# Four parts of the second layer's modulation are computed in the second layer's mixing in place of the first feed-forward

## The chip, the cores and the metric

The kernel runs on one core of one Trainium2 chip. The metric is the time of one execution on the device, in microseconds (us); lower is better. TensorE is PE, VectorE DVE, ScalarE ACT, GpSimd POOL and SyncE SP. PEld is the loading of weights into PE, beside its matmuls. Operands of PE are 32 bits wide.

## The reference, cut to what matters

Two layers work on a latent stream of 512 tokens and a context of 256, each token with 1024 features. A layer first makes six vectors per stream, its modulation, out of one small matrix product: SiLU(c) times a matrix of 1024 x 6144. Then it mixes tokens, and then it runs a feed-forward. The last layer does not update the context.

```python
sh_a, sc_a, ga_a, sh_f, sc_f, ga_f = ada_params(c, w_ada[i], b_ada[i])      # parts 0 to 5; likewise from c_ctx
h = rmsnorm(x, g_mix[i]) * (1.0 + sc_a) + sh_a                              # parts 1 and 0
y, yc = token_mixer(h, hc, ...)         # Fourier mixing, retention and neighbourhood attention, beside one another
x = x + ga_a * y                                                            # part 2
x = x + ga_f * swiglu(rmsnorm(x, g_ffn[i]) * (1.0 + sc_f) + sh_f, w1[i], w3[i], w2[i])    # parts 4, 3, 5
```

In the second layer parts 0 and 1 are needed for both streams, before its mixing starts. Parts 2 to 5 are needed for the latent stream alone: part 2 at its output projection, 3 and 4 at the norm of its feed-forward, 5 in the feed-forward's output.

## The kernel before, in words

Every large product is made three times, to keep 32-bit accuracy. Both operands are split into a high half in a reduced format (a cast on ACT) and a low half (the difference, on POOL or DVE), and PE adds high x high, low x high and high x low (`mm3`, lines 398 to 400). A weight chunk is thus loaded raw by SP, cast on ACT (line 183), subtracted on POOL or DVE (line 188), and only then used. The feed-forward uses a seven-product scheme on 2x2 blocks, so DVE also combines weight blocks (lines 225 to 229) and results (lines 1592 to 1658), and multiplies the two branches into the gated chunks `g` (lines 1634, 1635, 1461, 1462).

`WeightStream` is one list of all weights in the order of their use. It has buffers of one size: a raw chunk takes one, a split chunk of 1024 columns two, one of 512 columns one. `max_raws` limits the raw ones, `max_parts` the split ones and `SLOTS` their sum; 12 such buffers exist, and tables (rotary tables, attention bias, the SiLU tables) take the others. `issue` starts loads on SP's queue in the list's order while buffers are free. `split` handles the next entry; `get` hands a chunk to PE's work, and `done` frees it and lets the stream go on (`pump`). An entry can also be a unit of modulation: when its turn comes its raw buffer goes onto a list of waiting callbacks, and `flush`, which `get` calls, runs those whose time has come. That time is counted in planned PE time (`k.pe`). If the stream needs an entry that isn't issued yet, `flush(True)` runs all waiting callbacks at once.

For the second layer a unit is (part, i), a load of 512 KB with 128 of a part's 1024 features transposed onto partitions, and its callback `ada_dve` (lines 517 to 535) makes one pass on DVE per stream: multiply 128x1024 with the SiLU table of the stream, and sum (line 522, with an accumulator read behind it). After the eighth unit of a part the bias is added (`ada_bias`). For the first layer the products of parts 2 to 5 are made on PE (line 545), as units among the chunks of the first mixing.

`weights_of` (in `build`) places the units: `spread(units, lo, hi)` puts them evenly behind entries lo to hi of a layer's list. The list of the second layer's mixing has 37 chunks: four for the retention values (`rv`, 0 to 3), six for rotary queries and keys (`rq`, `rk`), three gates, six queries and keys and four values of the attention, two Fourier inputs, four transform tables, and eight output chunks (29 to 36).

The order of PE's work in the mixing is written out beforehand: `beside` interleaves the projections with the chain of retention (scores two items ahead of their values), readout and attention, by planned PE time and the offsets in `MIX`. Engines take their instructions in program order. In the retention each score tile goes from PE to DVE (times the decay, line 874), ACT (high half, line 931), DVE or POOL (low half, line 932) and back to PE. In the attention it goes through DVE (line 1076), ACT (exponential), DVE (lines 1118, 1119), PE (transpose), and ACT and DVE (lines 403, 404).

Of the kernel before, what the change touches and what calls it, by code (L numbers as in the profile page):

```python
# [14 lines left out]
NK = 8  # L15
# [24 lines left out]
DMA_WAIT = 8000.0  # L40
# [61 lines left out]
class WeightStream:  # L102
# [88 lines left out]
    def split(self):  # L191

        task = self.tasks[self.n_split]
        key, what, u = task
        size = self.need(task)
        if isinstance(what, Job):
            self.combine(what, key)
        else:
            raw = self.raw.pop(u)
            if what is not None:  # L200
                self.pending.append((what, raw, self.when[u] + DMA_WAIT if key[1] == 0 else 0.0))
            else:
                self.put(key, raw, raw.shape[-1])
                self.n_raw -= 1
            del raw
        self.size[key] = size
        self.n_parts += size
        self.n_split += 1
        self.issue()
# [101 lines left out]
def pieces(st):  # L311

    c0, n = st
    cut = min(max(NLAT - c0, 0), n)
    for s, lo, hi in ((0, 0, cut), (1, cut, n)):
        if hi > lo:
            yield s, slice(c0 + lo, c0 + hi), slice(lo, hi)
# [26 lines left out]
def run(*gens):  # L344
    for g in gens:
        for _ in g:
            pass


class Kern:  # L350
# [168 lines left out]
    def ada_dve(self, raw, layer, part, i):  # L519

        for s in range(1 if layer == DEPTH - 1 and part > 1 else 2):
            self.nc.vector.tensor_tensor_reduce(  # L522
                out=self.tmp(mybir.dt.bfloat16, D, "adj"),
                in0=raw,
                in1=self.tabs[("silu", s)],
                scale=1.0,
                scalar=0.0,
                op0=OP.mult,
                op1=OP.add,
                accum_out=self.mod[:, layer, part, s, i : i + 1],  # L530
            )
        if i == NK - 1:
            self.ada_bias(layer, part, lambda s: self.mod[:, layer, part, s, :])
            if (layer, part) == (DEPTH - 1, 5):
                self.tabs.clear()

    def ada(self, raw, part, half, u):
        nc = self.nc
# [497 lines left out]
    def na_evac_k(self, dst):  # L1036
# [14 lines left out]
        return f  # L1051

    def neighbours(self, layer, nqk, v, y, with_ctx, spans, nv_time, finish):

        nc = self.nc
# [130 lines left out]
        for i in range(len(items) + lag):  # L1186
            if i < len(items):
                h, b = items[i]
                if b == 0:
                    if h % 2 == 0:  # L1190
                        yield spans[h // 2] + (per,)
                        y[h // 2] = self.act(name="yn")
                    begin(h)
                yield score(h, b)
            if SL <= i < len(items) + SL:
                scale(*items[i - SL])
            if i >= lag:
                h, b = items[i - lag]
                if b == 1 and h > 0:
                    if h == 1:  # L1200
                        yield (nv_time, spans[0][1], per / 2)
                    yield values(h - 1, False)
                    if with_ctx:
                        yield values(h - 1, True)
                    if h % 2 == 0:
                        finish(h // 2 - 1)
                    parts(0)
                yield transp(h, b)
                if b > 0 or h == 0:
                    parts(b)  # L1210
        yield values(5, False)
        if with_ctx:
            yield values(5, True)
        finish(2)
        head.clear()

# [96 lines left out]
            for ps, w, m, st in waiting:  # L1313
                yield from self.products(ps, w, src, st, order[a:b], order)

    def residual(self, keys, src, x, layer, part, streams, after, norm, order, n, waiting, hook=None, paces=(1, 2, 2, 2), raws=3):

        nc = self.nc

        def put(ps, m, st):  # L1320
            for s, sl, at in pieces(st):
                xs = x[m][:, sl]
                nc.vector.scalar_tensor_tensor(
                    xs, ps[:, at], self.mod[:, layer, part, s, m : m + 1], xs, op0=OP.mult, op1=OP.add
                )
            after(m, st)

        def one(w, m, st, last, steps=0):
            ps = self.ps("res")
            run(self.products(ps, w, src, st, order, order))  # L1330
            if steps:
                norm.step(steps)
            put(ps, m, st)
            if last:
                self.w.done(keys[m])

        held = {}
        late = waiting[-1][2] + 1
        for ps, w, m, st in waiting:
            if hook:  # L1340
                hook()
            run(self.products(ps, w, src, st, order[n:], order))
            put(ps, m, st)
            if st is streams[-1]:
                self.w.done(keys[m])
        waiting.clear()
        del ps, w
        for m in range(late, NK):
            w = self.w.get(keys[m])
            if hook:  # L1350
                hook()
            if m < 4:
                for st in streams:
                    one(w, m, st, st is streams[-1])
            else:
                one(w, m, streams[0], False)
                held[m] = w
        self.w.max_raws = raws
        nc.scalar.activation(self.warm, self.eps, AF.Sqrt)
        for (m, w), n in zip(held.items(), paces):  # L1360
            one(w, m, streams[1], True, n)


class FeedForward:
# [351 lines left out]
    def finish(self, after, norm, hook=None):  # L1716

        k, q = self.k, len(self.parts) - 1
        size = self.parts[q][1]
        g = [[self.chunk(q, i, p) for i in range(2 * size)] for p in range(2)]  # L1720
        k.w.spare = 0
        k.w.max_raws, k.w.max_parts = 3, 8
        keys = [("w2", self.layer, q, m) for m in range(NK)]
        order = sorted(range(2 * size), key=lambda i: i % size == size - 1)
        waiting = []
        run(k.residual_ahead(keys, 3, g, self.out, order, [2 * size - 2], waiting, hook))
        k.residual(keys, g, self.x, self.layer, 5, self.out, after, norm, order, 2 * size - 2, waiting, hook)
        self.big = self.more = None


def build(tc, a, out, ctx, dbg=None, opts=None):
    k = Kern(ctx, tc, a, out, dbg)
# [5 lines left out]
    w = k.w = WeightStream(k, 3, 8)  # L1738
# [3 lines left out]
    def weights_of(layer):  # L1742
        lat_only = layer == DEPTH - 1
        main, between = [], {}

        def add(n, *idx, ap=None):
            main.append(((n, layer) + idx, a["w_" + n][(layer,) + idx] if ap is None else ap))

        for u in range(4):
            add("rv", u)  # L1750
        for c in range(3):
            add("rq", c)
            add("rk", c)
        for c in range(3):
            add("rg", c)
        for c in range(3):
            add("nq", c)
            add("nk", c)
            if c == 0:
                for u in range(4):  # L1760
                    add("nv", u)
        for c in range(2):
            add("f", c)
        for t in range(5 - lat_only):
            add("dft", t, ap=a["dft"][t] if t < 4 else a["dftc"])
        for m in range(NK):
            add("out", m)
        n_mix = len(main)

        def spread(units, lo, hi):  # L1770
            for i in range(lo, hi):
                n = len(units) * (i - lo) // (hi - lo), len(units) * (i + 1 - lo) // (hi - lo)
                between.setdefault(i, []).extend(units[n[0] : n[1]])

        steps = ffn[layer].order
        if layer == 0:
            spread([(layer, p, u) for p in range(2, 6) for u in range(NK)], 6, n_mix - 4)
        if layer + 1 < DEPTH:
            spread([(layer + 1, p, u) for p in range(6) for u in range(NK)], n_mix + 30, n_mix + len(steps) - 18)
        for i, (key, ap) in enumerate(main):  # L1780
            w.add(key, ap)
            for q in between.get(i, []):
                k.ada_unit(*q)
        for i, (job, p) in enumerate(steps):
            ffn[layer].add_weights(job, p)
            for q in between.get(n_mix + i, []):
                k.ada_unit(*q)
# [8 lines left out]
    x = [k.act(name="x") for _ in range(NK)]  # L1796
# [75 lines left out]
    for layer in range(DEPTH):  # L1872
        last = layer == DEPTH - 1
# [12 lines left out]
        for i, _ in enumerate(k.proj_v([("rv", layer, u) for u in range(4)], h, rv, norms, 3 if layer else 6)):  # L1886
            k.pe += 3 * 384 * NCOL
            if layer == 0 and i % 4 == 1:
                next(strips)
        w.SLOTS = 10  # L1890
        qk, nqk, u, wf = {}, {}, [None] * 2, []
        y, yn = [None] * 8, [None] * 3
        ysp = [[None] * 8, [None] * 8]
# [68 lines left out]
        outs, order, waiting = [("out", layer, m) for m in range(NK)], (2, 3, 4, 0, 1, 5, 6, 7), []  # L1962
# [48 lines left out]
        x = []  # L2011
# [236 lines left out]
```

## Time and profile before

| | us |
|---|---|
| three runs: lowest, median, highest | 1699.99, 1701.46, 1704.0 |
| the profiled execution, its own time | 1700.14 |
| its span, first to last instruction | 1698.4 |
| PE busy in the span | 1601.1 (94%) |
| DVE busy in the span | 1178.8 (69%) |
| POOL, ACT busy | 818.6 (48%), 741.9 (44%) |

The first layer's mixing ends near 450 us, its feed-forward runs to about 980, the second layer's mixing from there to about 1310, and the second feed-forward to the end. The second layer's modulation passes on DVE run from 532.6 to 928.2 us. The mean granted clock of TensorE over the span is 0.982 of full speed. A share of busy time over the whole span mixes stages with different limits, so the rows below go by stretches.

### The profile page before, as it was taken

To read this page: it belongs to the slowest core of one execution; us is meant where nothing else is said; L and a number is where in the kernel's file an instruction comes from. 1 tells how busy PE (TensorE), PEld (TensorE's weight loads), DVE (VectorE), ACT (ScalarE), POOL (GpSimd) and SP (SyncE) were. 2 spreads that over 40 slices of the span, in tenths; PEclk is the share of its full clock that TensorE was granted. 3 is DMA by queue.
4 is the path that set the end of the run, shared out by engine and by line. 5 is a ranking of instruction groups with operands and counts; after the bars stand their busy time and mean duration, and the time that the engine had idled before them with its cause. 6 is when DMAs were issued, how large, how long until landed. Compare 5 with 4: busy or idle time off the path is not lost. (4 is left out here: it accounts for less than half of the span.)

```text
span 1698.4 us, 26272 instructions
## 1 busy us (share of the span) xinstructions
PE 1601.1 (94%) x9730; PEld 1449.0 (85%) x9730; DVE 1178.8 (69%) x2054; ACT 741.9 (44%) x1437; POOL 818.6 (48%) x601
## 2 busy tenths in 40 slices
PE   6989999999979998999999999999999799999996
PEld 4867788888979987899999997779789789999996
DVE  6866566773777899586766776665666876766685
ACT  5534444653553223242332554444554544344343
POOL 3443232123375556465555623444125676666672
PEclk9999999999989999999999999999999899999998
DMA  9364253353023343434443345422232132332322
GB/s 355 139 199 138 67 160 97 119 170 130 26 76 111 103 134 120 129 125 137 149 137 118 127 161 163 135 73 74 80 131 81 60 115 75 111 114 76 94 87 69
DMA packets 76384, 202.28 MB, mean 119 GB/s; under 512 B 12704, under 2 KB 19488, under 8 KB 75872
## 3 DMA queue, kind: packets, MB, share of 16 engines
q1 hardware_dynamic: 76256, 200.60, 36.5%
q8 instruction: 77, 1.26, 0.3%
q14 instruction: 51, 0.42, 0.1%
HBM read 184.25 MB, written 11.80 MB: 115 GB/s over the span
## 5 line engine op out<-in xcount | busy, mean ns | idle before, releaser
L188 POOL TENSOR_TENSOR wp<-wr,wp 128x512 fp32r<-128x512 f32 (+1 forms) x336 | 465.7, 1399 | 311.0 <-ACT wp L183 306.2
L398 PE MATMUL f<-hp,wp 128*128 128x384 f32 (+1 forms) x1232 | 386.8, 314 | 14.8 <-DVE U L1599 4.2
L399 PE MATMUL f<-hp,wp 128*128 128x384 f32 (+1 forms) x1232 | 387.1, 314 | 10.8 <-DVE wp L188 6.2
L400 PE MATMUL f<-hp,wp 128*128 128x384 f32 (+1 forms) x1232 | 385.2, 313 | 4.0 <-POOL hp L1524 4.0
L183 ACT CAST wp<-wr 128x512 fp32r<-128x512 f32 (+1 forms) x360 | 213.3, 609 | 309.4 <-PE f L400 118.5
L188 POOL TENSOR_TENSOR wl<-wr,wh 128x1024 fp32r<-128x1024 f32 (+2 forms) x75 | 163.8, 2188 | 346.4 <-ACT wh L183 266.4
L398 PEld LDWEIGHTS f<-hp,wp 128*128 128x128 f32 x1232 | 238.0, 193 | 18.8 <-issue 8.2
L399 PEld LDWEIGHTS f<-hp,wp 128*128 128x128 f32 x1232 | 238.4, 193 | 15.3 <-POOL wp L188 8.5
L400 PEld LDWEIGHTS f<-hp,wp 128*128 128x128 f32 x1232 | 238.1, 193 | 5.1 <-POOL hp L1524 5.1
L398 PE MATMUL proj<-h,wh 128*128 128x512 f32 (+1 forms) x456 | 165.0, 362 | 1.0 <-DVE v L404 1.0
L398 PE MATMUL f<-g,wp 128*128 128x512 f32 (+1 forms) x468 | 160.5, 343 | 5.4 <-ACT g L1461 5.4
L400 PE MATMUL f<-g,wp 128*128 128x512 f32 (+1 forms) x468 | 160.5, 343 | 0.0
L399 PE MATMUL f<-g,wp 128*128 128x512 f32 (+1 forms) x468 | 160.3, 342 | 0.0
L399 PE MATMUL proj<-h,wl 128*128 128x512 f32 (+1 forms) x456 | 159.1, 349 | 0.7 <-POOL wl L188 0.7
L400 PE MATMUL proj<-h,wh 128*128 128x512 f32 (+1 forms) x456 | 158.9, 348 | 0.0
L1658 DVE SCALAR_TENSOR_TENSOR x<-f,mod,x 128x512 f32<-128x512 f32 (+1 forms) x130 | 79.0, 622 | 69.5 <-PE f L400 69.3
L398 PEld LDWEIGHTS proj<-h,wh 128*128 128x128 f32 x456 | 86.6, 190 | 25.5 <-issue 6.6
L522 DVE CUSTOM_DVE_ANT_0 adj<-wr,tab 128x1024 bf16<-128x1024 f32 x64 | 104.6, 1653 | 4.1 <-DMA wr<-in_w_adat_dram 4.0
L398 PEld LDWEIGHTS f<-g,wp 128*128 128x128 f32 x468 | 89.1, 190 | 17.0 <-ACT g L1461 6.8
L400 PEld LDWEIGHTS f<-g,wp 128*128 128x128 f32 x468 | 88.9, 190 | 11.2 <-DVE g L1462 1.1
L399 PEld LDWEIGHTS f<-g,wp 128*128 128x128 f32 x468 | 89.1, 190 | 9.9
L399 PEld LDWEIGHTS proj<-h,wl 128*128 128x128 f32 x456 | 86.8, 190 | 11.8 <-POOL wl L188 1.1
(251 smaller groups left out, 3415.2 us busy)
## 6 DMA issues: line engine op xcount, KB each, us to landing
wr<-in_w_dram SPq DMA_DIRECT2D x88, 512.0 KB
wr<-in_w_adat_dram SPq DMA_DIRECT2D x48, 512.0 KB
wr<-in_w_dram SPq DMA_DIRECT2D x80, 256.0 KB
wr<-in_w_ada_dram SPq DMA_DIRECT2D x32, 512.0 KB
ada<-in_w_ada_dram SPq DMA_DIRECT2D x16, 512.0 KB
wr<-in_w_out_dram SPq DMA_DIRECT2D x16, 512.0 KB
tab<-in_rpb_dram SPq DMA_DIRECT2D x12, 512.0 KB
strip<-strips SPq DMA_DIRECT2D x3, 1152.0 KB
```

The source lines that it names most:

```text
L183: nc.scalar.copy(hi, src)
L188: (nc.vector if vector else nc.gpsimd).tensor_sub(lo, src, hi.bitcast(F32))
L398: mm(out, a[0], b[0], start=start, stop=False)
L399: mm(out, a[1], b[0], start=False, stop=False)
L400: mm(out, a[0], b[1], start=False, stop=stop)
L522: self.nc.vector.tensor_tensor_reduce(out=self.tmp(mybir.dt.bfloat16, D, "adj"), in0=raw, in1=self.tabs[("silu", s)], scale=1.0, scalar=0. ...
L1658: k.nc.vector.scalar_tensor_tensor(xs, ps[:, :n], k.mod[:, self.layer, 5, s, m : m + 1], xs, op0=OP.mult, op1=OP.add)
```

## The change

The second layer's 32 units of parts 2 to 5 are placed behind chunks 6 to 32 of its own mixing, and only the 16 units of parts 0 and 1 stay in the first feed-forward, over the same range of entries as the 48 before. A unit of parts 2 to 5 waits for 8000 ns of planned PE time after its load's issue, as those of the first layer do. The context's SiLU table is released after part 1, the latent one after part 5, whose callback also raises `SLOTS` by one. Since that table now lives through the second mixing, the stream gets 10 slots and two raw buffers, in place of 11 and three, from the end of the first feed-forward to the end of the second layer's value projection, and 9 in place of 10 (with three raw buffers) in the second mixing.

```diff
--- before.py
+++ after.py
@@ -198,7 +198,7 @@
         else:
             raw = self.raw.pop(u)
             if what is not None:
-                self.pending.append((what, raw, self.when[u] + DMA_WAIT if key[1] == 0 else 0.0))
+                self.pending.append((what, raw, self.when[u] + DMA_WAIT if key[1] == 0 or key[2] > 1 else 0.0))
             else:
                 self.put(key, raw, raw.shape[-1])
                 self.n_raw -= 1
@@ -531,8 +531,11 @@
             )
         if i == NK - 1:
             self.ada_bias(layer, part, lambda s: self.mod[:, layer, part, s, :])
+            if part == 1:
+                del self.tabs["silu", 1]
             if (layer, part) == (DEPTH - 1, 5):
-                self.tabs.clear()
+                del self.tabs["silu", 0]
+                self.w.SLOTS += 1
 
     def ada(self, raw, part, half, u):
         nc = self.nc
@@ -1313,7 +1316,7 @@
             for ps, w, m, st in waiting:
                 yield from self.products(ps, w, src, st, order[a:b], order)
 
-    def residual(self, keys, src, x, layer, part, streams, after, norm, order, n, waiting, hook=None, paces=(1, 2, 2, 2), raws=3):
+    def residual(self, keys, src, x, layer, part, streams, after, norm, order, n, waiting, hook=None, paces=(1, 2, 2, 2), raws=2):
 
         nc = self.nc
 
@@ -1719,7 +1722,8 @@
         size = self.parts[q][1]
         g = [[self.chunk(q, i, p) for i in range(2 * size)] for p in range(2)]
         k.w.spare = 0
-        k.w.max_raws, k.w.max_parts = 3, 8
+
+        k.w.max_raws, k.w.max_parts, k.w.SLOTS = (3, 8, 11) if self.last else (2, 8, 10)
         keys = [("w2", self.layer, q, m) for m in range(NK)]
         order = sorted(range(2 * size), key=lambda i: i % size == size - 1)
         waiting = []
@@ -1773,10 +1777,9 @@
                 between.setdefault(i, []).extend(units[n[0] : n[1]])
 
         steps = ffn[layer].order
-        if layer == 0:
-            spread([(layer, p, u) for p in range(2, 6) for u in range(NK)], 6, n_mix - 4)
+        spread([(layer, p, u) for p in range(2, 6) for u in range(NK)], 6, n_mix - 4)
         if layer + 1 < DEPTH:
-            spread([(layer + 1, p, u) for p in range(6) for u in range(NK)], n_mix + 30, n_mix + len(steps) - 18)
+            spread([(layer + 1, p, u) for p in range(2) for u in range(NK)], n_mix + 30, n_mix + len(steps) - 18)
         for i, (key, ap) in enumerate(main):
             w.add(key, ap)
             for q in between.get(i, []):
@@ -1887,7 +1890,7 @@
             k.pe += 3 * 384 * NCOL
             if layer == 0 and i % 4 == 1:
                 next(strips)
-        w.SLOTS = 10
+        w.max_raws, w.SLOTS = 3, 9 if last else 10
         qk, nqk, u, wf = {}, {}, [None] * 2, []
         y, yn = [None] * 8, [None] * 3
         ysp = [[None] * 8, [None] * 8]
```

## Rows read from the trace of the kernel before

**Rows 1.** The page's totals: engine, busy us (share of the span), instructions.

```profile
span 1698.4 us, 26272 instructions
...
PE 1601.1 (94%) x9730; PEld 1449.0 (85%) x9730; DVE 1178.8 (69%) x2054; ACT 741.9 (44%) x1437; POOL 818.6 (48%) x601
```

**Rows 2.** Busy us by stretch: PE, PEld, DVE, ACT, POOL; granted clock; DMA.

```profile
530.00:590.00 60.00, 60.00 (x347) 56.08 (x346) 48.03 (x70) 15.91 (x29) 28.44 (x21) 1.00 0.37 118
590.00:690.00 100.00, 90.14 (x472) 81.69 (x471) 87.69 (x134) 32.42 (x65) 58.17 (x40) 0.97 0.42 135
690.00:930.00 240.00, 240.00 (x1389) 228.88 (x1388) 167.26 (x257) 75.51 (x138) 134.57 (x92) 1.00 0.41 130
...
1022.00:1125.00 103.00, 97.72 (x449) 76.17 (x448) 71.72 (x103) 44.49 (x72) 42.40 (x28) 1.00 0.38 122
1125.00:1275.00 150.00, 141.99 (x860) 127.29 (x859) 93.85 (x203) 81.09 (x159) 45.92 (x39) 0.98 0.31 99
1275.00:1310.00 35.00, 34.45 (x288) 34.36 (x288) 20.47 (x37) 17.52 (x38) 20.19 (x14) 1.00 0.27 92
```

**Rows 3.** The same table for line 522 (a modulation pass) alone.

```profile
530.00:590.00 60.00, 22.24 (x28) 1.00 0.37 118
590.00:690.00 100.00, 37.28 (x42) 0.97 0.42 135
690.00:930.00 240.00, 45.52 (x58) 1.00 0.41 130
```

**Rows 4.** Waits of PE, 595 to 722 us: total us, times, longest.

```profile
PE f L399 <- POOL wp L188: 4.3, 6, 0.9
PE f L398 <- ACT g L1461: 3.5, 2, 1.8
PE f L398 <- ACT wp L183: 2.0, 2, 1.0
```

**Rows 5.** Waits of PE, 1022 to 1275 us, the second mixing.

```profile
PE nav L1152 <- ACT pt L403: 2.1, 2, 1.7
PE rav L400 <- POOL ral L932: 2.0, 3, 0.7
PE nt L1130 <- DVE ne L1119: 1.9, 1, 1.9
```

**Rows 6.** Line 522, whole trace: ns min/median/max; who waited, us, times.

```profile
L522 DVE CUSTOM_DVE_ANT_0 adj<-wr,tab x64: 1204/1546/2375, 532.6 to 928.2; 128x1024 bf16<-128x1024 f32 x64
L522 DVE DVE_READ_ACCUMULATOR2_ANT mod<- x64: 73/77/85, 533.8 to 929.3; 128x1 f32 x64
...
  ACT wp L183: 41.1, 17
```

**Rows 7.** Who waited for line 522 from 690 to 930 us.

```profile
  ACT wp L183: 22.6, 11
```

**Rows 8.** Splits (line 183), 60 to 400 us: idle before, by releaser.

```profile
  DMA wr<-in_w_nk_dram: 1.9, 1
...
  DMA wr<-in_w_out_dram: 0.7, 1
  DMA wr<-in_w_rg_dram: 0.5, 1
```

**Rows 9.** One load's issue on SP; the cast on ACT that waited for it.

```profile
1017.51 0.33 SPq L145 DMA_DIRECT2D wr<-in_w_rk_dram  x1
...
1021.15 1.05 ACT L183 CAST wh<-wr 128x1024 fp32r<-128x1024 f32 x1 [1.93 <-DMA wr<-in_w_rk_dram]
```

**Rows 10.** Two pieces of the chain that ended last: start, us, what.

```profile
1309.41 0.65 DVE sq L597
...
1311.30 1.62 DVE wr L226
```

**Rows 11.** Low halves on POOL, 530:690 and 1022:1275: count, busy, mean.

```profile
L188 POOL TENSOR_TENSOR wp<-wr,wp 128x512 fp32r<-128x512 f32 x47 | 71.4, 1529 | 56.7 <-ACT wp L183 56.5
...
L188 POOL TENSOR_TENSOR wl<-wr,wh 128x1024 fp32r<-128x1024 f32 x20 | 48.4, 2426 | 53.6 <-ACT wh L183 31.5 <-PE res L399 12.2 <-ACT v L403 5.5
```

## The prediction

> **What bounds the kernel now.** I read the page's totals first, then the table of busy time by stretch, then who waited for whom in the stretches that the change touches, and last single instructions. The totals [rows 1] show VectorE at 69% of the span, so it binds only in places. In the stretches [rows 2] the reader is to compare PE with DVE. In the first feed-forward PE is busy 60.00 of 60 us with DVE at 80% (48.03 of 60), then only 90.14 of 100 us with DVE at 88%, then 240.00 of 240 with DVE at 70%. The modulation's own share of DVE [rows 3] is 22.24 of 60, 37.28 of 100 and 45.52 of 240 us. So PE starves where the two-stream units (parts 0 and 1, two operations each) come thickest, and PE's waits there are for the gate chain (ACT g behind DVE) and for split weights (ACT wp, POOL wp) [rows 4]. The 240 us after that are bound by PE alone.
>
> The second layer's mixing is another matter: PE is busy 97.72 of 103 and 141.99 of 150 us with DVE at 70% and 63% [rows 2]. Its stalls are many and short, and they end with results that come through DVE: the low halves of the retention scores and the softmax tiles [rows 5].
>
> **The change part by part.** One unit is a 512 KB load on SP and, per stream, one pass of 128x1024 on DVE with a short accumulator read, 1.64 us in all (the three numbers of rows 3, 105.04 us, over 64 passes) [rows 3, 6].
>
> *Removed from the first feed-forward.* 32 units, each with one pass: 32 x 1.64 = 52 us of DVE and 32 loads (16.8 MB) on SP. The 16 units that stay have 32 passes, 52 us, and the same range of steps as the 48 before, about 400 us; they are one in about 25 us in place of one in 8. In the starved 100 us DVE falls from 87.69 to 87.69 - 37.28 + 52/4 = 63 us. That is under the 70% at which PE lost nothing in the following 240 us. What PE can get back there is its idle time, 100 - 90.14 = 9.86 us, and the time at the lower clock: the granted clock was 0.97 on average, so 90.14 x 0.03 = 2.7 us. Upper end 12.6 us. Lower end: the two waits for ACT g (3.5 us) and the clock time behind them (2.7 us) stand at the ends of a part, where the gate chain is serial with or without modulation; if they stay, 6.4 us are left. The ends of the later parts lie inside the 240 us without idle time, so I take 11. The loads that go free nothing: the DMA engines are 41% busy there, and no wait for a load is in the row.
>
> *Added to the second layer's mixing.* The 32 units stand behind weight chunks 6 to 32 of 37. The last five stand behind the first four output chunks and come only with the output projection; about 27 passes, 27 x 1.64 = 44 us, fall in 1022 to 1275 us. They follow the chunks, so about 11 (18 us) in the first 103 us and 16 (26 us) in the other 150. DVE goes to (71.72 + 18)/103 = 87% and (93.85 + 26)/150 = 80%. No row shows what that costs in mixing. The nearest ones are those of the feed-forward: at 80% PE lost nothing, at 88% it lost 12.6 of 100 us. Lower end 0 (work added on DVE gives no time back), upper end 12.6% of all 253 us, 32 us. At 80% I take nothing for the second part. At 87% the row gives 13 us for the first part, but there each unit was two passes in a row, some 3.3 us in front of the next evacuation, and here it is one; the retention runs two items behind its scores, and other projections lie between. I take a little under half, 5 us. What waits behind a pass on DVE is the next evacuation; ACT waits for DVE too, since a split weight may need the buffer that the pass has just read (41.1 us in 17 waits in the feed-forward, 22.6 of them where PE lost nothing) [rows 6, 7].
>
> *The new wait of 8 us of planned PE time* (`key[2] > 1`) holds the pass until the next weight is fetched after it, and takes away most of the risk that DVE stands in front of a load that has not landed. It changes nothing for the units left in the feed-forward (parts 0 and 1).
>
> *Slots.* The stream has 9 in place of 10 in the second mixing. Three split chunks (6 slots) and three raw ones make 9 either way, so depth is not lost to the limit but to the units: of three raw buffers, about half now hold modulation. SP has one more load per chunk between its small copies and tables. The first layer's mixing runs just so (32 units of 512 KB, three raw buffers), and there the splits waited for a load 1.9, 0.7 and 0.5 us [rows 8]. Nothing for this; its ends are 0 and those 3.1 us.
>
> *Two raw buffers and 10 slots at the end of the first feed-forward and in the value projection.* The second layer's third and fourth projection chunks are then loaded one buffer's turn later, when a split has freed it. Now the load issued at 1017.51 us lets its cast start at 1021.15, 3.6 us on, after 1.93 us of waiting [rows 9]. Two such waits then stand in front of the evacuation of the values on ACT; PE has two of eight PSUM banks free, two whole products of 24 matmuls, before it needs that. 0 to 7 us, taken 0.5.
>
> *The last units in the output projection.* When the first output chunk is done the stream wants a unit that is not yet issued, so it runs all waiting passes: DVE stands for one load of some 3.6 us and does three passes, about 9 us in all, and the fifth output chunk is loaded behind two more units. DVE is busy 20.47 of 35 us there [rows 2], and PSUM banks cover PE, so most of it is absorbed before 1309 us; but from there until 1320 us the chain that ended last runs on DVE [rows 10]. 0 to 9 us, taken 1. Part 5, which is last, is first used after that, in the feed-forward's own output.
>
> *The sum:* -11 + 5 + 0.5 + 1 = -4.5 us against the profiled execution's own 1700.14 us (span 1698.4): 1695.6. The median of the runs shown, 1701.46, is 1.3 us above that execution, so 1697.0.
>
> **The rivals.** *A: the passes are free in the mixing.* DVE idles 30 to 37% of it, and a pass that falls in a gap delays nothing. For it: 80% with no loss in the feed-forward. Against: PE's stalls there already end with DVE results. Then only the 1.5 us of the edges are paid: -9.5, 1692.
>
> *B: the retention becomes bound by VectorE.* In 1022 to 1125 us DVE at 87% leaves 13 us of gaps in 103, while each retention item takes three turns (DVE, ACT, DVE or POOL) before PE can go on. If those turns can't fill the gaps, PE loses the full 13 us of the feed-forward's rate in this part, and at half that rate 9.5 us in the other: 22.5 + 1.5 against 11, +13, 1714; with the first part alone, 13 + 1.5 - 11 = +3.5, 1705. It is slower than before from 9.5 us of loss in the mixing on. For it: the many short stalls that are there already, and that POOL's passes in the mixing are longer, 2.43 us for a low half of 128x1024 against 1.53 us for one of 128x512 in the feed-forward [rows 11], so that a pass can be held longer. The pass took 1.204 us at best and 2.375 at worst [rows 6], about one short POOL pass more.
> The Trainium skill ("SBUF — State Buffer", section "SBUF: two separate sides") says that a VectorE operation with two SBUF inputs and a GpSimd operation that reads SBUF lock one pair of ports in turn, for a whole instruction. The trace's two durations agree with that; by that rule a pass in the mixing could take 1.2 + 2.4 = 3.6 us at worst; 11 such would give DVE 71.72 + 40 = 111 us of work in the 103, 8 us over, near this rival's smaller price, 1705.
>
> *C: the starvation in the feed-forward is the part's own.* Then only 6.4 us come back against 6.5 us paid: no change, 1701.5. Against it: the later parts end without a stall under 19% modulation. That the change doesn't do what it says is not to be feared: where a unit runs is set by its place in the stream.
>
> **How the numbers follow.** My forecast 0.42, its own range 1693 to 1701 (gain 9 to 12.6, mixing 3 to 7); rival A 0.14; rival B 0.30; rival C 0.14. The likeliest is the forecast, 1697.0. The range 1688 to 1711 leaves out the better end of A and the worse half of B, together no more than 0.2. A measurement of this kernel tells 0.2% (3.4 us) from no change, so faster is below 1698.1 and slower above 1704.9. Faster: two thirds of the forecast (0.29), all of A (0.14) and 0.03 of C, 0.46. Slower: 0.26 of B and 0.03 of C, 0.29. The same: 0.25.
>
> **What would show it.** In the feed-forward stretch that had 9.86 us idle PE should be busy throughout at full clock with DVE near 63%, and the second mixing should start about 11 us sooner. The mixing should last some 5 us longer, with DVE at 80 to 90% and more waits of PE for the low halves of the retention scores. I am wrong if the mixing lengthens by 9.5 us or more, if PE still waits for ACT g near the end of the first two parts, or if the splits wait for loads at the start of the second layer.

## The result: slower by 1.4%, and the profile after

The changed kernel took 1726.76 us (median of four runs, 1726.01 to 1730.18), the kernel before 1702.73 us (1699.99 to 1705.2) on the same chip. The ratio is 1.014, 95% interval 1.0122 to 1.0158. I had forecast 1697.0 with a range to 1711: wrong in sign, and outside the range. The profiled execution after took 1730.18 us, and its totals, which answer to [rows 1], are:

```profile
span 1728.4 us, 26269 instructions
PE 1614.2 (93%) x9730; PEld 1456.7 (84%) x9730; DVE 1181.5 (68%) x2054; ACT 742.4 (43%) x1437; POOL 814.7 (47%) x601
```

The work is the same, 2054 DVE and 9730 PE instructions. PE is busy 13 us longer in them than before (1614.2 against 1601.1), and 17 us more are idle. The profiled executions of the two kernels are 30 us apart and the medians 24, so the sections below overstate the loss by some 6 us.

To find the place, I cut both spans at the first or last matmul of a named tile: the first `f<-hp` of each feed-forward, the first `v` of the second layer, the first `rs`, the last `rav` (these two bound the retention), and so on through the mixing. The sections in us:

| | first mixing | first feed-forward | values | retention | readout | attention (`ns` to `fp`) | Fourier (`fp` to `res`) | `res` to second feed-forward | second feed-forward |
|---|---|---|---|---|---|---|---|---|---|
| before | 448.0 | 546.5 | 42.9 | 84.6 | 26.5 | 86.1 | 18.9 | 54.1 | 390.8 |
| after | 451.3 | 530.0 | 44.5 | 104.6 | 28.1 | 98.6 | 21.9 | 60.1 | 389.3 |

The first feed-forward is 16.5 us shorter. The second mixing, from the values on, is 357.8 us instead of 313.1: 44.7 us longer, 20.0 of them in the retention and 12.5 in the attention. The first mixing is the same code in all kernels here and took 448.0 to 453.6 us, so a difference of 5 us in that section means nothing; the retention took 84.6 to 85.3 us in the seven kernels that left it alone, so there 1 us does. The whole second mixing took 312.8 to 316.0 us in these seven (in four of them the readout ran at a granted clock of 0.94 and took 28.1 us), so a difference of 3 us in it means nothing either.

The table by stretch, columns as in [rows 2]: two stretches of the first feed-forward after the change, then the retention and the attention by the bounds of the sections, each before and after, so that a pair holds the same matmuls:

```profile
530.00:590.00 60.00, 60.00 (x347) 56.08 (x347) 34.10 (x54) 16.91 (x31) 29.92 (x22) 1.00 0.26 82
590.00:690.00 100.00, 100.00 (x575) 95.76 (x574) 72.04 (x111) 35.82 (x69) 58.08 (x45) 1.00 0.35 107
...
1037.40:1122.00 84.60, 80.06 (x361) 61.42 (x359) 61.30 (x84) 36.62 (x57) 37.57 (x25) 1.00 0.37 119
...
1025.80:1130.40 104.60, 88.02 (x360) 64.95 (x360) 79.22 (x107) 38.60 (x59) 40.00 (x25) 0.93 0.46 149
...
1148.50:1234.60 86.10, 81.95 (x474) 72.99 (x474) 52.65 (x128) 44.63 (x94) 22.73 (x21) 0.96 0.25 79
...
1158.50:1257.10 98.60, 86.24 (x474) 75.11 (x473) 69.53 (x154) 43.84 (x92) 25.95 (x22) 0.93 0.42 127
```

The reader is to see three things. The 100 us that had 9.86 us of PE idle are full, at full clock. DVE is busy 72% there, and not the 63% that I had worked out, since 575 matmuls in place of 472 fit into them. In the retention PE is idle for 16.58 of 104.6 us, before for 4.54 of 84.6, and yet DVE is idle too, for 25.4 us: busy 76%, before 72%, and not the 87% that I had worked out for a slightly wider stretch, since the stretch itself became longer. And the granted clock fell from 1.00 to 0.93 in the retention and from 0.96 to 0.93 in the attention: in parts of these stretches PE ran at the lower of its two levels, 1.2 GHz, after its stalls (from 1100 to 1110 us, around the stall shown below, the granted clock was 0.66). For the same matmuls PE is busy 8.0 us longer in the retention and 4.3 us in the attention. So of the 20.0 us that the retention lost, 12.0 are idle time of PE and 8.0 are slower matmuls; over the whole mixing, by the same cut, 26.7 and 18.0.

PE's waits from 1025 to 1290 us, against [rows 5] (us in total, times, longest):

```profile
PE rav L398 <- ACT rah L934: 11.6, 7, 4.8
PE res L399 <- POOL wl L188: 4.6, 2, 3.4
PE rav L400 <- POOL ral L935: 3.5, 6, 0.7
PE nt L1133 <- DVE ne L1122: 2.9, 2, 2.0
```

The first line is new as a large one (before: 1.3 us in 2 times). ACT, which makes `rah`, waits in its turn for DVE in the retention, after and before:

```profile
ACT rah L934 <- DVE ra L877: 36.8, 20, 5.6
...
ACT rah L931 <- DVE ra L874: 23.6, 19, 2.3
```

What DVE did meanwhile is seen in single instructions (start, us, what), here around one such wait of ACT and the wait of PE behind it, DVE, then ACT, then POOL, then PE:

```profile
1095.91 1.22 DVE L522 CUSTOM_DVE_ANT_0 adj<-wr,tab 128x1024 bf16<-128x1024 f32 x1
...
1097.18 2.19 DVE L585 TENSOR_TENSOR mod<-mod,vec 128x8 f32<-128x8 f32 x1
1099.29 1.21 DVE L522 CUSTOM_DVE_ANT_0 adj<-wr,tab 128x1024 bf16<-128x1024 f32 x1
...
1100.43 1.95 DVE L877 SCALAR_TENSOR_TENSOR ra<-rs,strip 128x512 f32<-128x512 f32 x2
...
1101.53 0.62 ACT L934 CAST rah<-ra 128x512 fp32r<-128x512 f32 x1 [4.81 <-DVE ra L877]
...
1096.30 3.04 POOL L188 TENSOR_TENSOR wl<-wr,wh 128x1024 fp32r<-128x1024 f32 x1 [0.91 <-ACT wh L183]
...
1102.20 0.74 PE L398 MATMUL rav<-rah,v 128*96 128x512 f32 x1 [4.79 <-ACT rah L934]
```

Two modulation passes and a bias add, 4.6 us together, stand on DVE in front of one score tile; ACT waits 4.81 us for that tile, and PE 4.79 us for ACT. The delay goes through the chain in full. About 2 us of it come from POOL: the bias add, 128x8, ends with POOL's subtraction.

The other side is the stream of weights. Splits on ACT (line 183) from 985 to 1330 us waited for their loads, by tensor:

```profile
  DMA wr<-in_w_f_dram: 5.8, 2
  DMA wr<-in_w_rq_dram: 4.1, 1
  DMA wr<-in_w_rk_dram: 3.3, 1
  DMA wr<-in_w_out_dram: 3.1, 1
  DMA wr<-in_w_dram: 2.4, 2
  DMA wr<-in_w_nq_dram: 1.1, 1
```

That is 19.8 us of ACT's time, which PE feels only where it waits behind ACT; before, it was 2.3 us. The loads are issued later. Of the kernel before, the first load for the gates and the first for the attention queries, on SP:

```profile
1024.72 0.33 SPq L145 DMA_DIRECT2D wr<-in_w_rg_dram  x1
...
1058.19 0.38 SPq L145 DMA_DIRECT2D wr<-in_w_nq_dram  x1
```

and of the kernel after:

```profile
1041.67 0.33 SPq L145 DMA_DIRECT2D wr<-in_w_rg_dram  x1
...
1086.40 0.53 SPq L145 DMA_DIRECT2D wr<-in_w_nq_dram  x1
```

The second is 28 us later, in a kernel that began its mixing 13 us earlier. Part of that is buffers that are still held. SP's queue, which issues all loads in order, waited from 1020 to 1300 us for modulation passes and bias adds (3.4 us of it between these two loads):

```profile
SPq L145 <- DVE mod L522: 17.7, 8, 5.1
...
SPq L145 <- DVE mod L585: 9.2, 2, 8.3
```

Before, there is no such wait in the mixing. Another part is the order of the queue: shortly ahead of the late load of the attention queries stands a copy of a rotary tile (line 1910) that waited 9.9 us for ACT.

### The profile page after: what moved, and what is told of

The parts are those of the page before. It is cut to its first block, busy times and chain, and to the rows that moved or that the text cites. A ratio compares the mean times of both kernels' runs of the same rounds, so it can differ in the third digit from the quotient of the medians.

```text
span 1728.4 us, 26269 instructions
## 1 busy us (share of the span) xinstructions
PE 1614.2 (93%) x9730; PEld 1456.7 (84%) x9730; DVE 1181.5 (68%) x2054; ACT 742.4 (43%) x1437; POOL 814.7 (47%) x601
## 5 line engine op out<-in xcount | busy, mean ns | idle before, releaser
L188 POOL TENSOR_TENSOR wp<-wr,wp 128x512 fp32r<-128x512 f32 (+1 forms) x336 | 454.6, 1365 | 302.7 <-ACT wp L183 297.4
L188 POOL TENSOR_TENSOR wl<-wr,wh 128x1024 fp32r<-128x1024 f32 (+2 forms) x75 | 169.5, 2264 | 365.5 <-ACT wh L183 337.1
L398 PE MATMUL proj<-h,wh 128*128 128x512 f32 (+1 forms) x456 | 167.1, 366 | 1.0 <-DVE v L404 1.0
L400 PE MATMUL proj<-h,wh 128*128 128x512 f32 (+1 forms) x456 | 161.0, 353 | 0.0
L398 PEld LDWEIGHTS proj<-h,wh 128*128 128x128 f32 x456 | 88.1, 193 | 25.9 <-issue 4.9
L522 DVE CUSTOM_DVE_ANT_0 adj<-wr,tab 128x1024 bf16<-128x1024 f32 x64 | 99.5, 1583 | 2.2 <-DMA wr<-in_w_adat_dram 2.1
L398 PEld LDWEIGHTS f<-g,wp 128*128 128x128 f32 x468 | 88.7, 190 | 13.6 <-ACT g L1464 3.5
L400 PEld LDWEIGHTS f<-g,wp 128*128 128x128 f32 x468 | 88.6, 189 | 11.0 <-DVE g L1465 0.8
L400 PEld LDWEIGHTS proj<-h,wh 128*128 128x128 f32 x456 | 87.7, 192 | 12.0
```

The lines of the kernel that those rows point to most:

```text
L188: (nc.vector if vector else nc.gpsimd).tensor_sub(lo, src, hi.bitcast(F32))
L398: mm(out, a[0], b[0], start=start, stop=False)
L400: mm(out, a[0], b[1], start=False, stop=stop)
L522: self.nc.vector.tensor_tensor_reduce(out=self.tmp(mybir.dt.bfloat16, D, "adj"), in0=raw, in1=self.tabs[("silu", s)], scale=1.0, scalar=0. ...
```

## The experiments

Twelve kernels were run, each timed against the kernel before on the same chip. Experiments 1 to 4 took the change apart; 6 to 9 separated what a moved unit costs in the mixing; 5 and 10 to 12 asked where the first feed-forward's gain came from. Line numbers shift by a few from kernel to kernel. In the diffs, `...` stands for edits or parts of lines that are left out.

**1. Short passes.** The changed kernel, parts 2 to 5 with passes of 8 columns.

```diff
+            w = 8 if layer == DEPTH - 1 and part > 1 else D
...
-                in0=raw,
-                in1=self.tabs[("silu", s)],
+                in0=raw[:, :w],
+                in1=self.tabs[("silu", s)][:, :w],
```

> The changed kernel, with the passes of parts 2 to 5 cut to 8 of 1024 columns; loads, slots and places stay (the rest of these sums is left out). Theory 1 (the passes stand on VectorE in front of score and softmax evacuations, and PE waits for the chain behind them): nearly all of the loss in the mixing goes, 1726.8 falls to 1686 to 1697. Theory 2 (the 32 loads take raw buffers and SP's turns, so splits and copies come late): stays at 1718 to 1727. If each has a part, in between: 1700 to 1715.

Measured: 1701.12 us, ratio 0.9983 (0.9968 to 0.9999). The retention took 93.1 us and the whole second mixing 332.8, 19.7 more than before. Splits waited for loads as in the changed kernel (21.5 us from 985 to 1330 us). Cutting the passes took away 25.0 of the mixing's 44.7 us, so DVE's time in them is the larger part of the loss. But some 20 us stay, and the short passes are not free:

```profile
L523 DVE CUSTOM_DVE_ANT_0 adj<-wr,tab x32: 153/163/2141, 1023.4 to 1281.1; 128x8 bf16<-128x8 f32 x32
```

The median is 0.16 us, the longest 2.14, and together they keep DVE busy for 14.7 us. So the 19.7 us are not the loads and buffers alone.

**2. Small loads.** The changed kernel, parts 2 to 5 with loads of 8 columns and whole passes over a broadcast column.

```diff
-            self.w.add(("ada", layer, part, i), self.a["w_adat"][q], callback=...
+            u = self.a["w_adat"][q]
+            self.w.add(("ada", layer, part, i), u if part < 2 else u[:, :8], callback=...
...
```

> The changed kernel, with the loads of parts 2 to 5 cut from 1024 to 8 columns (one of them is read 1024 times over, so these parts' values are others); the passes stay whole, as do slots and places. Theory 1 (passes): stays at 1718 to 1727. Theory 2 in the form that the 16.8 MB of loads themselves delay others: falls to 1690 to 1700. The raw buffers are still held, so the slot form of theory 2 is left by this.

Measured: 1724.4 us, 1.0122 (1.0098 to 1.0145). Retention 105.7, whole mixing 356.1. The interval overlaps that of the changed kernel, and the mixing is 1.7 us shorter, inside its spread of 3 us: no cost of the 16.8 MB themselves is seen. What is left of the loads is the raw buffer that each holds and its turn in SP's queue.

**3. The limits alone.** The kernel before with the changed limits and nothing moved.

```diff
-        w.SLOTS = 10
+        w.max_raws, w.SLOTS = 3, 9 if last else 10
```

(and the two other edits of limits, as in the change).

> The kernel before, with the stream's new limits alone (two raw buffers and 10 slots from the end of the first feed-forward to the end of the value projection, 9 slots in the second mixing); all 48 units stay in the first feed-forward. Theories 1 and 2: 1700 to 1706, as before. Theory 3 (fewer raw buffers and slots make splits late by themselves): 1708 or more.

Measured: 1706.43 us, 1.0 (0.9983 to 1.0017). The values took 43.4 and the retention 85.3 us. The two raw buffers and the 9 slots cost nothing that can be measured.

**4. The gain alone.** The kernel before with parts 2 to 5 of the second layer's modulation left out and constants in their place.

```diff
-            spread([(layer + 1, p, u) for p in range(6) for u in range(NK)], n_mix + 30, ...
+            spread([(layer + 1, p, u) for p in range(2) for u in range(NK)], n_mix + 30, ...
...
```

> The kernel before, with parts 2 to 5 of the second layer's modulation left out (constants in their place), the 16 units of parts 0 and 1 spread over the same range. It shows the first feed-forward's gain alone. My prediction: 11 us, 1691 to 1692. The changed kernel's trace (its first feed-forward is 16.5 us shorter there): 1686.

Measured: 1684.83 us, 0.9887 (0.9865 to 0.9909): 19 us, of which the first feed-forward shows 16.6 (529.9 us). This bounds what any other place for these units could bring. From here on I reckon from this kernel: the change costs 1.014 - 0.9887, 2.5% or 43 us, behind it.

**5. Even units.** The kernel before with its 48 units in another order: one of two passes, then two of one pass, all through.

```diff
+            both, one = ([(layer + 1, p, u) for p in ps for u in range(NK)] for ps in (range(2), range(2, 6)))
+            spread([x for i in range(16) for x in (both[i], one[2 * i], one[2 * i + 1])], n_mix + 30, ...
```

> The kernel before with its 48 units in another order in the same places: one unit of two passes (parts 0 and 1), then two of one pass (parts 2 to 5), and so on. The work is the same and stays in the first feed-forward. Theory 1 (PE starves there where passes come thicker than VectorE has room for): VectorE is then near 78% throughout, and most of the 19 us come back: 1684 to 1692. Rival (the passes cost PE by their number wherever they stand): 1698 to 1705.

Measured: 1705.88 us, 1.0018 (1.0003 to 1.0032); the first feed-forward took 550.7 us. PE's waits in it, 520 to 990 us:

```profile
PE f L398 <- ACT g L1461: 9.9, 3, 3.5
PE f L399 <- POOL wp L188: 3.4, 5, 0.9
```

Before there were two waits for `g`, between 590 and 690 us [rows 4]; now there are three, one each in 640 to 690, 740 to 790 and 840 to 890 us. From 690 to 930 us PE was busy 233.23 of 240 us with DVE at 72% (173.22 us), where before it lost nothing at 70%. So it was not the thickness of the two-pass units: thinning them moved the stalls.

**6. No passes.** The changed kernel with its loads, buffers and places, without the passes of parts 2 to 5.

```diff
-        for s in range(1 if layer == DEPTH - 1 and part > 1 else 2):
+        for s in range(0 if layer == DEPTH - 1 and part > 1 else 2):
...
```

> The changed kernel without the passes of parts 2 to 5 (constants in their place); their loads, raw buffers, slots and places stay. It divides the 16 us between the kernel with passes of 8 columns (1701) and the one with parts 2 to 5 left out (1685). If the units' raw buffers and turns in the stream cost that: 1698 to 1702. If even a pass of 8 columns costs it, by waiting for POOL's operation to end: 1684 to 1689.

Measured: 1691.98 us, 0.994 (0.9925 to 0.9955). Retention 90.0, whole mixing 322.3 us, 9.2 more than before. No instruction of an engine reads the raw buffers here, but the stream still counts each as held until the wait of 8 us is over. The time lies between the two ranges expected, so neither the buffers and turns nor the short passes alone make what is left in experiment 1.

**7. Passes alone.** The changed kernel with whole passes of parts 2 to 5 at their places, without load and raw buffer: they read the SiLU table twice. As nothing is loaded for them, they run without the wait of 8 us.

```diff
+            if part > 1:
+                self.w.tasks.append((("ada", layer, part, i), lambda raw: self.ada_dve(raw, layer, part, i), None))
+                return
...
-                in0=raw,
+                in0=self.tabs[("silu", s)] if raw is None else raw,
```

> The changed kernel with the passes of parts 2 to 5 whole and at the same places of the list, but with no load and no raw buffer of their own (they read the SiLU table twice, so their values are others). If passes and buffers add up, 1727 less some 16: 1708 to 1714. If the passes alone make the whole loss: 1720 to 1727.

Measured: 1713.35 us, 1.0066 (1.0049 to 1.0082). Retention 96.4, whole mixing 340.0 us, 26.9 more than before. PE's waits from 985 to 1330 us:

```profile
PE rav L398 <- ACT rah L937: 7.3, 6, 3.2
PE rav L400 <- POOL ral L938: 4.5, 6, 1.1
```

Without raw buffers held, splits waited for loads only 5.8 us, and the wait for `rah` stayed (in experiment 1, where the passes are short, it fell to 2.8 us). The 26.9 us are 15.4 us more idle time of PE and 11.5 us more busy time for the same matmuls. The costs do not simply add up: 26.9 us with the passes alone and 9.2 with the loads, buffers and wait alone (experiment 6) make 36.1, where the change itself made 44.7.

**8. Units behind chunk 13.** The changed kernel with the 32 units behind chunks 13 to 32 instead of 6 to 32.

```diff
-        spread([(layer, p, u) for p in range(2, 6) for u in range(NK)], 6, n_mix - 4)
+        spread([(layer, p, u) for p in range(2, 6) for u in range(NK)], 13 if lat_only else 6, n_mix - 4)
```

> The changed kernel with the 32 units placed behind chunks 13 to 32 in place of 6 to 32, so that most come after the retention. If a pass costs what it delays in the chain of the retention (20 us of the loss lie there): 1706 to 1714. If it costs the same anywhere in the mixing, and more where units come thicker: 1722 to 1735.

Measured: 1719.17 us, 1.0104 (1.0082 to 1.0127). The retention fell from 104.6 to 91.1 us, while the attention took 100.4 instead of 98.6. The whole mixing is 346.6 us, 11 less than with the change. Fewer passes in the retention cost less there, the attention lost 1.8 us more, and the version stays slower than the kernel before.

**9. Without the wait of 8 us.** The changed kernel with units of parts 2 to 5 run at the next fetch.

```diff
-... if key[1] == 0 or key[2] > 1 else 0.0))
+... if key[1] == 0 else 0.0))
```

> The changed kernel without the new wait of 8 us of planned PE time for parts 2 to 5. If the wait guards VectorE from loads that have not landed, as I predicted: slower than the changed kernel, 1732 or more. If it costs, since it holds raw buffers that weights need (9 us are lost with the units' buffers and no passes): 1716 to 1722. If neither: 1724 to 1730.

Measured: 1715.49 us, 1.0076 (1.0061 to 1.0091): 11 us less than with the wait. Values 49.7 us (with the wait 44.5), retention 94.2 (104.6), whole mixing 345.6 (357.8). PE's waits from 985 to 1330 us:

```profile
PE rs L398 <- ACT rk L749: 7.2, 2, 6.2
PE rav L398 <- ACT rah L934: 4.9, 4, 3.2
PE rav L400 <- POOL ral L935: 3.7, 5, 1.1
```

Where the wait is gone, the beginning is worse by 5.2 us (the first line), and the rest is better by 17.4. Splits waited 12.2 us for loads instead of 19.8. Experiment 7 differs from this one by the loads and raw buffers alone, as neither has the wait: its mixing is 5.6 us shorter (340.0), and its ratio 1.0066 in place of 1.0076, with intervals that overlap. So without the wait, the loads and buffers cost little, and in the whole time nothing clear of noise.

**10. Two-stream parts last.** The kernel before with the order of parts 2, 3, 4, 5, 0, 1.

```diff
+            spread([(layer + 1, p, u) for p in (2, 3, 4, 5, 0, 1) for u in range(NK)], n_mix + 30, ...
...
```

> The kernel before with its 48 units in another order in the same places of the first feed-forward: parts 2 to 5 (one pass each) first, parts 0 and 1 (two passes each) last. With the even order the stalls moved to three ends of parts, where PE waits for the gate chain. If two passes in a row are harmless except at the second part, which has one chunk where others have two and comes in the first third: 1685 to 1694. If they cost at every end of a part: 1697 to 1706.

Measured: 1706.62 us, 1.0022 (1.0009 to 1.0035); first feed-forward 550.3 us, with PE waiting for `g` once in 640 to 690 and once in 840 to 890 us:

```profile
PE f L398 <- ACT g L1461: 10.4, 2, 6.7
```

**11. The passes of a unit apart.** The kernel before; the second pass of a two-stream unit runs one fetch later than the first.

```diff
+            more = callback(raw)
+            if more is not None:
+                self.pending.append((more, raw, 0.0))
...
```

> The kernel before with the two passes of a unit of parts 0 and 1 apart: the second stream's pass runs at the next fetch of a weight. If it is the length of what stands in front of the gate chain (3.3 us against 1.6): 1685 to 1694. If it is VectorE's load near the ends of parts, or the raw buffers (held longer here): 1698 to 1708.

Measured: 1704.92 us, 1.0006 (0.9993 to 1.0018); first feed-forward 546.1 us. The time did not move, and from 590 to 690 us PE was busy 90.65 us, as before.

**12. Passes alone in the first feed-forward.** The kernel before, its units of parts 2 to 5 without load and raw buffer, as in experiment 7.

> The kernel before with the 32 units of parts 2 to 5 at their old places in the first feed-forward, but without load and without raw buffer: their passes, of the same size, read the SiLU table twice. This leaves a part of the computation out. It says what in those units costs the first feed-forward the 16.6 us that came back when they were left out (546.5 to 529.9 us, total ratio 0.989). Theory 1, the passes' time on VectorE: the feed-forward stays at 543 to 548 us, ratio 0.998 to 1.002, and PE still waits for ACT g. Theory 2, the raw buffers that they hold and the loads in SP's queue: the feed-forward falls to 530 to 534 us, ratio 0.989 to 0.992. Both in like parts: 537 to 540 us, ratio 0.995.

Measured: 1703.56 us, 1.0006 (0.9996 to 1.0016); first feed-forward 546.7 us, PE's wait for `g` 4.7 us in 3 times. In the first feed-forward the loads and buffers of these units cost nothing that can be measured; so the 16.6 us of experiment 4 are their passes'.

## Why the prediction was wrong, step by step

**What bounds the kernel.** The reading was right in its parts: PE starved in the first feed-forward, and in the mixing its many short stalls ended with results that come through DVE. What I did not draw from it is that this second kind of stall does not ask how busy DVE is.

**Removed from the first feed-forward (-11, bounds 6.4 to 12.6).** Right in direction, too small: the stage gave 16.5 us, and 16.6 in experiment 4. All idle time and all clock loss of the 100 us came back. The whole first feed-forward, before and after:

```profile
448.00:994.50 546.50, 523.53 (x2932) 492.66 (x2932) 419.27 (x634) 201.43 (x381) 310.13 (x220) 0.98 0.37 117
...
451.30:981.30 530.00, 516.31 (x2933) 490.57 (x2932) 371.14 (x564) 201.11 (x380) 298.33 (x220) 0.99 0.28 88
```

PE has 9.3 us less of idle time, about the 9.86 of the forecast, and is busy 7.2 us less for the same matmuls, where the forecast had 2.7 for the clock: this term was too small. The reason given with it, that the two-stream units come thickest there, fell: evened out, put last or taken apart, they gave no gain (experiments 5, 10, 11). With 64 passes the stalls came back in each order that I tried, in one place or another; with 32 they were nearly gone (PE waited for `g` behind ACT once, 0.6 us). So in these orders it was the number of passes that counted. Why 64 stall PE and 32 do not is not shown.

**Added to the second layer's mixing (+5, bounds 0 to 32).** This is the larger failure: 26.9 us by experiment 7, near the end that I had named and did not take. The step carried a rule from the feed-forward, "at 80% PE lost nothing", into a stage with another limit. Here each score tile goes PE, DVE, ACT, DVE or POOL, PE, and a pass that lands in front of a tile delays it by its length, as the lines above show for one tile, whatever the share of DVE that is idle afterwards. 32 passes of at least 1.2 us are 39 us, and the mixing lost 26.9: about 0.8 us for each, the slower matmuls behind the stalls included. "Two items behind its scores" was not cover enough for several in a row, and experiment 5 shows that the rule did not even hold in the feed-forward: with DVE at 72%, PE lost 6.8 of 240 us.

**New wait of 8 us (cost 0, protective).** Wrong in sign. It does protect the first units, 5.2 us in the values' stage; then it costs 17.4 us (experiment 9), 12.2 net. A raw buffer whose load has landed is kept until the pass may run, and DVE gets passes together more often: 19 of the 32 in the mixing stand directly behind or in front of another one, without the wait 12. Which of the two makes the 17.4 us was not tried.

**Slots (0, ends 0 to 3.1).** Too small, most of all together with the wait. Loads and raw buffers cost 5.6 us of mixing without the wait (experiments 9 and 7), 9.2 with the wait and nothing that reads the buffers (experiment 6), and 17.8 with the wait and the whole passes (the change against experiment 7). Between experiments 6 and 1 lie 10.5 us, which I can't divide: the buffers are held until DVE comes to its pass, and the short passes themselves take 14.7 us of DVE. I had seen the cause ("of three raw buffers, about half now hold modulation") and priced it by the first layer's mixing, where the splits waited 3.1 us [rows 8]. There the units are read by PE, and here they wait for DVE; that this makes the difference was not tried. The loss of look-ahead showed where I had said it would, in splits that wait for loads, 19.8 us of ACT's time; how much of that reached PE was not followed.

**Two raw buffers and 10 slots (+0.5).** By themselves nothing (experiment 3). After the change two splits of the first projections waited 4.1 and 3.3 us for their loads, and the values' stage took 1.6 us longer, 44.5 us; with the same limits it took 42.8 to 44.3 in experiments 1, 2, 3, 6 and 8, so this is no sure loss.

**Last units in the output projection (+1, 0 to 9).** The stretch from `res` to the second feed-forward lost 6.0 us: inside its ends, and larger than taken. With passes and no loads it lost 0.5 (experiment 7), with loads and no passes nothing (experiment 6), and with both but without the wait of 8 us 0.5 (experiment 9). So neither the three passes nor the loads cost it, but the units that the wait heaps up, as the step said.

**The rivals.** A and C fell: the mixing did not take the passes for nothing, and no wait of PE is left from 595 to 722 us. B came nearest, with the sign right and its price of 1714 still 13 us short of the time. Its headline, a retention bound by VectorE, is not what happened: DVE was idle a quarter of the retention. Its ground, that each item takes three turns before PE can go on and that these can't fill the gaps, is the mechanism that the runs support. The rule of the Trainium skill ("SBUF — State Buffer", section "SBUF: two separate sides") agrees with the trace here:

```profile
1059.90 3.22 DVE L522 CUSTOM_DVE_ANT_0 adj<-wr,tab 128x1024 bf16<-128x1024 f32 x1
...
1059.65 2.39 POOL L188 TENSOR_TENSOR wl<-wr,wh 128x1024 fp32r<-128x1024 f32 x1
```

The pass ends at 1063.12, 1.08 us after POOL's operation ended at 1062.04. But few passes meet one: 9 of the 32 in the mixing took more than 1.4 us, and all took 50.4 us, 11.4 us above 32 of 1.22 us. How much of the 26.9 us is due to it was not measured by itself.

**What is settled, and what is not.** Settled: 16.5 us gained; of the 44.7 us lost in the mixing, 26.9 come with the passes alone, 5.6 more with their loads and raw buffers, and 12.2 more with the wait, each step with up to 3 us of spread. In another order of steps the shares are others: on top of loads, buffers and wait the passes cost 35.5 us (experiment 6). No version with the whole computation beat the kernel before; the best with units in the mixing was experiment 9, at 1.0076. Not settled: what each stage's loss is made of beyond the retention, where I followed single waits, and why the wait costs what it does.

## What to carry to other kernels

Where an engine stands inside a serial chain of short turns, its idle share is not room: price work put on it at its own length for each piece, and the slower matmuls behind the stalls with it, until a trace of that stage shows otherwise, and take a rule on "busy share without loss" only from a stage with the same limit. A moved unit that brings a load also takes a buffer from the look-ahead of the stream, from the load's issue to the last reader; a wait that keeps a landed buffer is to be tried by itself. And measure the gain by itself first (the units left out): here it was 1.1%, the most that another place for these units could have brought.

## What the runs showed of the hardware that I had not expected

POOL's subtraction held up a tiny DVE operation as it did the pass above. The bias add of 128x8 took 166 ns at its shortest and 2383 ns at its longest in the mixing:

```profile
L585 DVE TENSOR_TENSOR mod<-mod,vec x4: 166/1178/2383, 1097.2 to 1307.4; 128x8 f32<-128x8 f32 x4
```

The one at 1097.18 us ended at 1099.37, with POOL's low half, which ended at 1099.34. And stalls of a few us each went with a second cost: in the retention PE was idle for 12.0 us more, and at a granted clock of 0.93 in place of 1.00 the same matmuls took 8.0 us more (88.02 against 80.06).
